# Expert numbers by one wide mask in place of sixteen compare-sums, in a three-block kernel on one core

## The chip, the cores and the metric

The kernel runs on one core of a Trainium2 chip. The core has five engines that run their own instruction streams in order: TensorE (PE in the rows, with PEld for its weight loads), VectorE (DVE), ScalarE (ACT), GpSimd (POOL) and SyncE (SP, which starts most transfers). The metric is the device time of one execution in microseconds, as the median of several runs.

## What is computed

Three blocks of a sequence model run one after the other on 512 tokens of 1024 features, in float32. The change lies in the second block, in the choice of experts. A token has 8 heads; each head scores 128 keys twice, keeps the 16 best of either list, forms all sums of two, keeps the 16 best sums, and turns their places into numbers of experts out of 16384. Each expert is a row of `peer_u` and a row of `peer_v`.

```python
v1, i1 = lax.top_k(s1, PEER_TOPK)          # 16 of 128 keys
v2, i2 = lax.top_k(s2, PEER_TOPK)
cand = (v1[..., :, None] + v2[..., None, :]).reshape(T, PEER_HEADS, PEER_TOPK * PEER_TOPK)
cand_id = (i1[..., :, None] * N_KEYS + i2[..., None, :]).reshape(T, PEER_HEADS, PEER_TOPK * PEER_TOPK)
score, pos = lax.top_k(cand, PEER_TOPK)
ids = jnp.take_along_axis(cand_id, pos, axis=-1)
gates = jax.nn.softmax(score, axis=-1)
...
act = jax.nn.gelu(jnp.einsum('pd,phkd->phk', hb, expert_u[ib]))
return jnp.einsum('phk,phkd->pd', gb.astype(hb.dtype) * act, expert_v[ib])
```

## The kernel before

The 512 tokens are four tiles of 128, taken in two halves of two tiles. The halves run one behind the other: while half 0 is with its experts, half 1 goes through the first two blocks; while half 1 is with its experts, half 0 goes through the third block. So the experts of a half always run beside dense products of the other half.

**Routing.** `peer_route` (L1061) makes the scores of a half, two heads at a time, with products on TensorE. `route_steps` (L1242) holds what follows for two heads of a token tile. `first` (L1252) calls `top16` (L1232) for each key list: a search for eight largest (L1235), their places (L1236), the list without them (L1238, into the tile `mrep`), and the same once more (L1239, L1240). `cands` (L1267) converts the places to float32 (L1273), multiplies those of the first list by 128 (L1276) and forms the 50 sums of two that can be among the 16 best, first of the values, then of the numbers: nine additions for each (L1281, L1284), over two heads at once or over one. `second` searches the 16 best of the 50 sums and their places. `ids` (L1301) finds the numbers: for each of the 16 places k, one instruction (L1303) compares the row 0..49 (`io`) with the place, multiplies by the 50 numbers and leaves the sum over the columns in an accumulator, which a second small instruction reads. L1306 converts the 16 numbers into `idx`. `soft` makes the gates. All of these are on DVE but an exponential on ScalarE. There are 32 heads in all (8 heads, 4 token tiles), so 512 compare-sums, and 18 calls of `cands` (14 for two heads, 4 for one).

**Experts.** `gather_steps` (L1155) makes 256 steps for a token tile. `fetch` (L1164) lets GpSimd start an indirect transfer of 128 rows of 4 KB, with the numbers from one column of `idx`; up to eight are under way ahead of their use. A step with a row of `peer_u` is a product-sum of 1024 columns on DVE (L1171); a step with a row of `peer_v` is a multiply-add of 1024 columns on DVE (L1194) or, for a share of them, two products on TensorE (L1188).

**What sets the order.** The steps of routing and experts are a list (`self.fill`), merged at even rates. Phases of the other half call `tick` with an amount of work, and steps are let in as a credit grows; a step of the routing counts 0.8, one of the experts 1.46, as before and after the change. Within that, a scheduler of the framework orders the instructions of every engine by its own estimate of durations, so the order on an engine moves when instructions become longer or fewer.

Of the kernel before, what the change touches and what calls it, by code (L numbers as in the profile page):

```python
# [19 lines left out]
P = 128  # L20
T = 512
NT = 4          # token tiles
NH = 2          # token tiles of a half: the halves run one behind the other
# [11 lines left out]
# Costs of steps, in the unit of tick and idle: a transfer of 512 KB, a step of the routing, the end of a token tile  # L35
DMA, ROUTE, FINISH = 1.46, 0.8, 6.0
AHEAD = 8           # gathers under way ahead of their use
GB = 15             # their buffers
# the hidden blocks of the feed-forwards that run piece by piece in the gaps of the other half
ASIDE1 = (4, 4, 4, 4, 4, 2)  # L40
ASIDE3 = (4,) * 4
FIRST3 = 16          # hidden blocks of the third feed-forward of half 0 beside the last experts
ADA = 28             # tiles of the modulation beside the first feed-forward, the others beside the second
CONV_PE = (0, 2)     # blocks of the long convolution on TensorE, by half
# by phase: pace of the steps of the experts, share of their sums that TensorE takes
ZONE = dict(x=(1, 0.5), g=(1, 0.35), h=(1.15, 0.41), c=(0.43, 0.4), f=(1.43, 0), m=(1.73, 0.06), d=(1.09, 0.4),
            R=(1.09, 0.39), r=(1.33, 0.3), F3=(1.1, 0), s=(1, 0.65))
# pieces let in by gap of TensorE
GAP = dict(_0=4, l=3, h=0.74, c=0.22, m=5.53, d=0.9, r=0.5, s=1.6, _4=5.2, ln=8, l4=8)
NORM = 4.82          # pace of a normalisation  # L50
WEIGHTS = 3          # of a tile of weights in float32
# rates of the steps: modulation beside the two feed-forwards, experts during the routing
RATE_ADA, RATE_ROUTE = (0.85, 0.6), (0.92, 2.17)
# the course of the phases beside the experts, the transfers of their own, and the share of the experts' steps to fit in
# [3 lines left out]
class Ker:  # L58
    def __init__(self, ctx, tc, I):
# [3 lines left out]
        self.exact = False      # products in float32 itself, not in parts  # L63
# [14 lines left out]
        self.aux = nc.gpsimd        # for what VectorE need not do, unless GpSimd has transfers to start  # L78
# [3 lines left out]
        # states: of the first and of the second block, then both of the third block's retention  # L82
# [13 lines left out]
    def xt(self, es, side=None):  # L96
        """transposed activations, split in two, for one phase"""
        xp = es.enter_context(self.tc.tile_pool(name="xt", bufs=1, side=side))
        self.XH, self.XL = self.pair(xp, "X", KD)

    def pair(self, pool, name, n, **k):
        """an operand of products, n blocks: in two parts, or whole"""
        if self.exact:
            return pool.tile([P, n, TH], F32, name=name + "H", **k), None
        return [pool.tile([P, n, TH], F32R, name=name + c, **k) for c in "HL"]
# [19 lines left out]
    def course(self, i):  # L125
        """the rate that spreads the steps of the experts over a phase"""
        whole, loads, share = COURSE[i]
        self.rate, self.credit = (share * sum(f[0] for f in self.fill) + loads) / whole, 0.0

    def tick(self, d, load=0.0):  # L130
        """a phase goes on by d, with load for a transfer of its own: the steps of the other half's experts
        go in between so that the transfers are even"""
# [12 lines left out]
    def idle(self, d):  # L145
        """TensorE has little to do for d: pieces of the feed-forward set aside go in between"""
        if self.side is not None:
            self.lull += d
            while self.lull > 0.0 and self.side is not None:
                self.lull -= self.next_piece()  # L150
# [25 lines left out]
    def rsqrt(self, out, in_, scale, eps):  # L176
        """out = (in_ * scale + eps) ** -0.5: Newton's iteration from the halved exponent"""
# [43 lines left out]
    def ahead(self):  # L221
        """of the weights of a feed-forward set aside, split the next tile and load on"""
# [9 lines left out]
    def whole(gen):  # L232
        """all pieces of a generator at once; its value"""
# [12 lines left out]
    def g_fm(self, srcs):  # L246
        """feature-major blocks: out[f, i, t] = sum_k w_i[k, f] X[t, k]; srcs [128, 8*128]"""
# [16 lines left out]
    def g_tm(self, srcs, lhs, evac):  # L264
        """token-major: out[t, c] = sum_k lhs[k, t] w[k, c]; srcs: list of [128, 2, 512]; lhs(k) -> (H, L) [128, 512]"""
# [23 lines left out]
    def stats(self, y):  # L289
        """mean and variance over the free axis (1024 or 512)"""  # L290
# [12 lines left out]
    def g_transpose_x(self, src, scale=None, bias=None):  # L303
        """XH, XL <- split of (src^T * scale + bias); src(t, k) -> [128 t, 128 feat]"""
# [18 lines left out]
    def layer_norm(self, gname, bname, alpha):  # L323
        """x <- alpha * LN(x); XT <- split of LN(x)^T"""
# [35 lines left out]
    def g_ffn(self, parts, up, down, scale, fb=0):  # L360
        """x += scale * ffn; up(pool, j): generator of blocks j and j + 1 of the hidden layer, [128, 2, TH];
        down(k, c): weights of blocks k and k + 1"""
# [164 lines left out]
    def _hgrn(self, hp, uT, acc):  # L527
# [5 lines left out]
        # lower bound: softmax over the two rows, first row  # L533
# [128 lines left out]
    def ada_setup(self):  # L662
        """modulation vectors, feature-major: mod[:, 8*i + k] = feature 128*k + p of the i-th of six"""
# [24 lines left out]
    def wide(self, pool, name, key, n=D, at=0):  # L688
        """a row on all partitions; where transfers hold the time, from its columns on TensorE"""
# [6 lines left out]
    def bcast_row(self, out, colsv):  # L696
        """out[*, 128*k + p] = colsv[p, k]"""
# [18 lines left out]
    def g_rms_xt(self, xn, scale, bias):  # L716
        """xn[t] <- x * rstd; XT <- split of (xn^T * scale + bias)"""
# [29 lines left out]
    def softplus(self, pool, z, n):  # L747
        """z <- log(1 + exp(z)), accurate for any z"""
# [17 lines left out]
    def gemm_narrow(self, pool, src, n, meta=None):  # L766
        """token-major X @ w[:, :n] -> psum [128, (t, n)]; src [128, 8*n]; with the meta tokens from 256 on"""
# [22 lines left out]
    def _mixer2(self, mp):  # L790
# [5 lines left out]
        # q, k, v: short convolution and silu, feature-major  # L796
# [32 lines left out]
    def put_mix(self, blk, t, src, nb=4, dst=None):  # L829
        """XH, XL blocks blk.. of token tile t <- split of src^T (src token-major [128, nb*128])"""  # L830
# [41 lines left out]
    def delta_gates(self, dp, ab):  # L872
        nc, I = self.nc, self.I
        # g = -exp(a_log) * softplus(a + dt_bias), beta = sigmoid(b)
# [13 lines left out]
    def _delta(self, dp, qkv, zz, g, bt):  # L888
# [12 lines left out]
        eg = dp.tile([P, 3, NH, 4], F32, name="eg")   # exp of the sums of g: up to here, all, after here  # L901
# [6 lines left out]
        for t in range(NH):  # L908
# [30 lines left out]
            # decay, transposed: DT[j, i] = exp(sum of g over j < tau <= i) for j <= i, else 0  # L939
# [18 lines left out]
            # q exp(gc) feature-major; k exp(total - gc), kb exp(gc) token-major  # L958
# [11 lines left out]
            # X = (I + A)^-1 by doubling over block sizes, with its transpose  # L970
# [28 lines left out]
            # u = X (v beta);  wT = -(X (kb exp(gc)))^T  # L999
# [37 lines left out]
    def head_norm(self, pool, po, gate, blk, t, dst=None):  # L1037
        """XT blocks blk..blk+3 of tile t <- (rms over each head of 128) * gate"""
# [13 lines left out]
    CW = [16 // (i + 1) for i in range(16)]     # of the sorted sums v1[i] + v2[j] only (i + 1)(j + 1) <= 16 can lead  # L1052
# [8 lines left out]
    def peer_route(self, rate):  # L1061
        """experts and gates of this half; leaves in self.fill the steps that gather and apply them"""
# [7 lines left out]
        with ExitStack() as e2:  # L1070
# [7 lines left out]
            # before the first gathers GpSimd has time  # L1078
# [37 lines left out]
            def each(sc, h):  # L1116
                # the first head of the first tile at once, so that its gathers start
# [21 lines left out]
        # the choice for two heads more beside the products of the heads before  # L1139
# [3 lines left out]
        # the last sums of the first tile beside the first products of the second  # L1143
# [6 lines left out]
    def merge(a, b):  # L1150
        """the two lists of steps, in between one another at an even rate"""
# [3 lines left out]
    def gather_steps(self, t, y, h2, idx, gate):  # L1155
# [72 lines left out]
        # those that the first 2, 4, 6 and 8 heads allow  # L1228
# [3 lines left out]
    def top16(self, src, val, idx, n):  # L1232
        """the 16 largest of src [128, n] with their places, in order"""
# [3 lines left out]
        w = self.sm.tile([P, P], F32, tag="mrep", name="mrep", bufs=2)  # L1237
# [4 lines left out]
    def route_steps(self, g, sc, idx, gate, early=False):  # L1242
        """expert numbers and gates of a token tile for heads 2g and 2g + 1, from their scores sc"""
# [3 lines left out]
        NC = self.NC  # L1247

# [7 lines left out]
        def begin():  # L1256
            w = pp.tile([P, 192 + 5 * NC], F32, name="rt", bufs=2)
            o = 0
            st["fx"] = w[:, 0:64].rearrange("p (h i) -> p h i", i=16)
            o = 64  # L1260
            for k, i in (("score", 16), ("pos", 16), ("fp", 16), ("fid", 16), ("cand", NC), ("cid", NC)):
                st[k] = w[:, o:o + 2 * i].rearrange("p (h i) -> p h i", i=i)
                o += 2 * i
            st["jk"] = w[:, o:o + NC]
            st["pos"] = st["pos"].bitcast(U32)

        def cands(h0, h1):  # L1267
            if h0 == 0:
                begin()
            n = h1 - h0  # L1270
            bs, hs = slice(2 * h0, 2 * h1), slice(h0, h1)
            val, fx, cand, cid = st["val"][:, bs, :], st["fx"][:, bs, :], st["cand"][:, hs, :], st["cid"][:, hs, :]
            nc.vector.tensor_copy(fx, st["ix"][:, bs, :])  # L1273
            v1, v2 = val[:, 0::2, :], val[:, 1::2, :]
            f1, f2 = fx[:, 0::2, :], fx[:, 1::2, :]
            nc.vector.tensor_scalar(f1, f1, 128.0, None, op0=ALU.mult)  # L1276
            for dst, a, b in ((cand, v1, v2), (cid, f1, f2)):
                o = 0
                for i in range(8):
                    w = self.CW[i]  # L1280
                    nc.vector.tensor_tensor(out=dst[:, :, o:o + w], in0=b[:, :, 0:w],  # L1281
                                            in1=a[:, :, i:i + 1].to_broadcast([P, n, w]), op=ALU.add)
                    o += w
                nc.vector.tensor_tensor(out=dst[:, :, o:o + 8], in0=a[:, :, 8:16],  # L1284
# [669 lines left out]
```

## Time and profile before

| | |
|---|---|
| median of three runs | 3475.92 us |
| the three runs | 3460.99, 3475.92, 3478.14 us |
| span of the profiled execution | 3464.7 us |
| mean granted TensorE clock | 0.932 of full speed |
| DMA over the span | 957.1 MB, mean 276 GB/s |

The profile gives the span of one execution, from its first to its last instruction, and no other time of that execution. Of the runs, one is shorter than this span and two are longer. [...] The accumulator's read stands as an instruction of its own (DVE_READ_ACCUMULATOR).

### The profile page before, as it was taken

To read this page: it belongs to the slowest core of one execution; us is meant where nothing else is said; L and a number is where in the kernel's file an instruction comes from. 1 tells how busy PE (TensorE), PEld (TensorE's weight loads), DVE (VectorE), ACT (ScalarE), POOL (GpSimd) and SP (SyncE) were. 2 spreads that over 40 slices of the span, in tenths; PEclk is the share of its full clock that TensorE was granted. 3 is DMA by queue.
4 is the path that set the end of the run, shared out by engine and by line. 5 is a ranking of instruction groups with operands and counts; after the bars stand their busy time and mean duration, and the time that the engine had idled before them with its cause. 6 is when DMAs were issued, how large, how long until landed. Compare 5 with 4: busy or idle time off the path is not lost. (4 is left out here: it accounts for less than half of the span.)

```text
span 3464.7 us, 44842 instructions
## 1 busy us (share of the span) xinstructions
PE 3023.7 (87%) x15402; PEld 2350.9 (68%) x15402; DVE 2667.9 (77%) x6456; ACT 1145.3 (33%) x1687; POOL 1439.0 (42%) x1187
## 2 busy tenths in 40 slices
PE   9999999998979789987777867879797975999998
PEld 9987889888866357836354643536474745888897
DVE  7779686665588999878898999897877786566555
ACT  4454544553312242103222121112222213455554
POOL 0020000023245656655677567586767671211200
PEclk9999999999999899998899988899998987999999
DMA  8863477542389979998999899999999995644365
GB/s 312 279 194 118 131 267 233 168 161 86 105 303 357 355 263 384 409 402 325 381 326 375 335 339 391 347 368 357 333 365 359 396 409 193 182 133 139 119 188 162
DMA packets 276757, 957.10 MB, mean 276 GB/s; under 512 B 38304, under 2 KB 42144, under 8 KB 276528
## 3 DMA queue, kind: packets, MB, share of 16 engines
q0 software_dynamic: 147456, 536.94, 41.0%
q1 hardware_dynamic: 129072, 417.29, 35.6%
q8 instruction: 122, 2.00, 0.2%
q14 instruction: 107, 0.88, 0.1%
HBM read 947.81 MB, written 2.10 MB: 274 GB/s over the span
## 5 line engine op out<-in xcount | busy, mean ns | idle before, releaser
L1164 POOL DMA_INDIRECT gu<-in_peer_v,idx x512 | 633.6, 1238 | 317.1 <-issue 111.9
L1164 POOL DMA_INDIRECT gu<-in_peer_u,idx x512 | 609.3, 1190 | 349.6 <-issue 110.9
L1171 DVE SCALAR_TENSOR_TENSOR gu<-gu 128x1024 f32<-128x1024 f32 x512 | 620.7, 1218 | 59.4 <-DMA gu<-in_peer_u,idx 55.7
L203 DVE TENSOR_TENSOR wL<-wr,wH 128x1024 fp32r<-128x1024 f32 x332 | 409.1, 1234 | 249.2 <-ACT wH L202 231.9
L256 PE MATMUL ps<-XH,wr 128*128 128x256 f32 x2368 | 528.7, 383 | 0.2 <-issue 0.2
L256 PEld LDWEIGHTS ps<-XH,wr 128*128 128x128 f32 x2368 | 450.9, 192 | 73.2 <-issue 12.8
L202 ACT CAST wH<-wr 128x1024 fp32r<-128x1024 f32 x332 | 348.3, 1050 | 440.3 <-PE ps L281 217.4
L1194 DVE SCALAR_TENSOR_TENSOR gu<-gu,act 128x1024 f32<-128x1024 f32 x366 | 467.6, 1278 | 28.6 <-DMA gu<-in_peer_v,idx 23.4
L1188 PE MATMUL ps<-gu,dg 128*128 128x512 f32 x568 | 306.5, 664 | 101.8 <-DMA gu<-in_peer_v,idx 67.4
L1188 PEld LDWEIGHTS ps<-gu,dg 128*128 128x128 f32 x568 | 112.7, 212 | 206.9 <-issue 158.2
L278 PE MATMUL ps<-wr,XH 128*128 128x512 f32 x512 | 229.1, 601 | 0.0
L256 PE MATMUL ps<-XH,wH 128*128 128x256 f32 x1408 | 206.5, 289 | 16.3 <-ACT XH L116 10.0
L256 PE MATMUL ps<-XH,wL 128*128 128x256 f32 x1408 | 202.4, 287 | 1.5 <-DVE wL L203 1.2
L256 PE MATMUL ps<-XL,wH 128*128 128x256 f32 x1408 | 203.0, 288 | 0.2
L256 PEld LDWEIGHTS ps<-XH,wH 128*128 128x128 f32 x1408 | 186.6, 196 | 21.9 <-ACT XH L116 13.7
L256 PEld LDWEIGHTS ps<-XH,wL 128*128 128x128 f32 x1408 | 185.6, 196 | 2.9 <-DVE wL L203 2.7
L203 DVE TENSOR_TENSOR fL<-fr,fH 128x1024 fp32r<-128x1024 f32 x98 | 126.1, 1288 | 79.5 <-ACT fH L202 50.1
L256 PEld LDWEIGHTS ps<-XL,wH 128*128 128x128 f32 x1408 | 186.5, 197 | 0.6 <-DVE XL L118 0.6
L278 PEld LDWEIGHTS ps<-wr,XH 128*128 128x128 f32 x512 | 98.0, 193 | 122.7 <-issue 120.3
L202 ACT CAST fH<-fr 128x1024 fp32r<-128x1024 f32 x98 | 102.6, 1047 | 175.4 <-PE ps L256 58.7
L1186 ACT ACTIVATE dg<-ident,act 128x128 f32<-128x128 f32 x142 | 55.1, 400 | 312.3 <-PE ps L1188 246.5
L184 POOL TENSOR_TENSOR r<-rx,mhalf 128x1 f32<-128x1 f32 x18 | 11.9, 669 | 330.7 <-DVE rx L182 330.7
(618 smaller groups left out, 5462.4 us busy)
## 6 DMA issues: line engine op xcount, KB each, us to landing
wr<-in_wi_fm SPq DMA_DIRECT2D x112, 512.0 KB
wr<-in_wi_tm SPq DMA_DIRECT2D x96, 512.0 KB
wr<-in_wf SPq DMA_DIRECT2D x96, 512.0 KB
wr<-in_wo SPq DMA_DIRECT2D x64, 512.0 KB
wa<-in_wada SPq DMA_DIRECT2D x48, 512.0 KB
wr<-in_f2g SPq DMA_DIRECT2D x44, 512.0 KB
wr<-in_f2u SPq DMA_DIRECT2D x44, 512.0 KB
wr<-in_f2d SPq DMA_DIRECT2D x44, 512.0 KB
```

The source lines that it names most:

```text
L184: nc.gpsimd.tensor_tensor(out=out, in0=x, in1=self.mhalf[:p, :].to_broadcast(list(out.shape)), op=ALU.pow)
L202: self.nc.scalar.copy(H, raw)
L203: self.nc.vector.tensor_tensor(out=L, in0=raw, in1=H, op=ALU.subtract)
L256: nc.tensor.matmul(ps[:, i * TH:(i + 1) * TH], a[:, k * P:(k + 1) * P], b[:, k, :], start=n == 0, stop=n == KD * len(terms) - 1)
L278: nc.tensor.matmul(pss[t], lh[:, ts], wh, start=k == 0, stop=k == nk - 1)
L1164: nc.gpsimd.indirect_dma_start(out=g, out_offset=None, in_=I[src], in_offset=bass.IndirectOffsetOnAxis(ap=idx[:, s:s + 1], axis=0))
L1171: nc.vector.scalar_tensor_tensor(g, g, 1.0, h2, op0=ALU.mult, op1=ALU.mult, accum_out=st["act"][:, s:s + 1])
L1186: nc.scalar.activation(dg, self.ident, AF.Copy, scale=c)
L1188: nc.tensor.matmul(st["ps"][i], dg, g[:, i * 512:(i + 1) * 512], start="pe" not in st, stop=s == 127)
L1194: nc.vector.scalar_tensor_tensor(st["acc"], g, c, st["acc"], op0=ALU.mult, op1=ALU.add)
```

## The change

`cands` converts the places in place (in the second half of the tile `rv`), so that values and places lie in one tile, and forms the sums of both by the same instruction: nine additions over twice the columns in place of eighteen. The results lie in one tile `cc`, values first, numbers second. `ids` makes a mask of 16 x 50 for a head by one comparison (the row 0..49 repeated for each place, against each place repeated over 50 columns), multiplies it by the 50 numbers repeated, and sums over the columns: three instructions over 800 columns (L1305, L1306, L1307 of the changed file) in place of sixteen pairs. The mask has one buffer (`eq`); the tile of the searches, `mrep`, has one buffer in place of two, and the scratch tile `rt` becomes smaller. Costs and tables that pace the steps are the same; the other lines of the diff are comments that went.

```diff
-        w = self.sm.tile([P, P], F32, tag="mrep", name="mrep", bufs=2)
+        w = self.sm.tile([P, P], F32, tag="mrep", name="mrep", bufs=1)
...
-            w = pp.tile([P, 192 + 5 * NC], F32, name="rt", bufs=2)
+            w = pp.tile([P, 128 + 4 * NC], F32, name="rt", bufs=2)
...
-            nc.vector.tensor_copy(fx, st["ix"][:, bs, :])
-            v1, v2 = val[:, 0::2, :], val[:, 1::2, :]
-            f1, f2 = fx[:, 0::2, :], fx[:, 1::2, :]
+            nc.vector.tensor_copy(rv[:, 1, bs, :], st["ix"][:, bs, :])
+            f1 = rv[:, 1, bs, :][:, 0::2, :]
             nc.vector.tensor_scalar(f1, f1, 128.0, None, op0=ALU.mult)
-            for dst, a, b in ((cand, v1, v2), (cid, f1, f2)):
-                o = 0
-                for i in range(8):
-                    w = self.CW[i]
-                    nc.vector.tensor_tensor(out=dst[:, :, o:o + w], in0=b[:, :, 0:w],
-                                            in1=a[:, :, i:i + 1].to_broadcast([P, n, w]), op=ALU.add)
-                    o += w
-                nc.vector.tensor_tensor(out=dst[:, :, o:o + 8], in0=a[:, :, 8:16],
-                                        in1=b[:, :, 0:1].to_broadcast([P, n, 8]), op=ALU.add)
+            both, dst = rv[:, :, bs, :], st["cc"][:, :, hs, :]
+            a, b = both[:, :, 0::2, :], both[:, :, 1::2, :]
+            o = 0
+            for i in range(8):
+                w = self.CW[i]
+                nc.vector.tensor_tensor(out=dst[:, :, :, o:o + w], in0=b[:, :, :, 0:w],
+                                        in1=a[:, :, :, i:i + 1].to_broadcast([P, 2, n, w]), op=ALU.add)
+                o += w
+            nc.vector.tensor_tensor(out=dst[:, :, :, o:o + 8], in0=a[:, :, :, 8:16],
+                                    in1=b[:, :, :, 0:1].to_broadcast([P, 2, n, 8]), op=ALU.add)
...
         def ids(h):
-            for k in range(16):
-                nc.vector.scalar_tensor_tensor(st["jk"], io, st["fp"][:, h, k:k + 1], st["cid"][:, h, :],
-                                               op0=ALU.is_equal, op1=ALU.mult, accum_out=st["fid"][:, h, k:k + 1])
+            eq = pp.tile([P, 16, NC], F32, name="eq", bufs=1)
+            wide = lambda a: a.rearrange("p (o j) -> p o j", o=1).to_broadcast([P, 16, NC])
+            fp = st["fp"][:, h, :].rearrange("p (k o) -> p k o", o=1).to_broadcast([P, 16, NC])
+            nc.vector.tensor_tensor(out=eq, in0=wide(io), in1=fp, op=ALU.is_equal)
+            nc.vector.tensor_tensor(out=eq, in0=eq, in1=wide(st["cc"][:, 1, h, :]), op=ALU.mult)
+            nc.vector.tensor_reduce(out=st["fid"][:, h, :], in_=eq, op=ALU.add, axis=AX.X)
```

DVE's order before, at the end of the first head of half 0 (`rt` holds sums, places and numbers, `rv` values and places of the keys, `sc` the scores, `idx` the numbers that the gathers read):

```order
L1289 CAST rt<-rt 128x16
L1303 SCALAR_TENSOR_TENSOR rt<-io,rt 128x50 x14
L1235 MAX rv<-sc 128x8
L1303 SCALAR_TENSOR_TENSOR rt<-io,rt 128x50
L1236 MAX_INDEX rv<-rv,sc 128x8
L1303 SCALAR_TENSOR_TENSOR rt<-io,rt 128x50
L1238 MATCH_REPLACE mrep<-rv,sc 128x128
L1306 CAST idx_9031<-rt 128x16
```

The same place on DVE in the changed kernel:

```order
L1288 CAST rt<-rt 128x16
L1305 TENSOR_TENSOR eq<-io,rt 128x800
L1306 TENSOR_TENSOR eq<-eq,rt 128x800
L1307 TENSOR_REDUCE rt<-eq 128x16
L1309 CAST idx_9031<-rt 128x16
L1235 MAX rv<-sc 128x8 x2
```

Sixteen compare-sums with three instructions of the next searches between them became three wide ones with nothing between.

DVE's order before, around the first expert step (L1171), which stands 62 rows behind the first head's numbers:

```order
L1303 SCALAR_TENSOR_TENSOR rt<-io,rt 128x50
L1240 MAX_INDEX rv<-rv,mrep 128x8
L1303 SCALAR_TENSOR_TENSOR rt<-io,rt 128x50
L1171 SCALAR_TENSOR_TENSOR gu,act<-gu 128x1024
L1303 SCALAR_TENSOR_TENSOR rt<-io,rt 128x50
```

The first expert step in the changed kernel, on DVE:

```order
L1236 MAX_INDEX rv<-rv,sc 128x8
L1240 MAX_INDEX rv<-rv,mrep 128x8
L1272 CAST rv<-rv 128x32
L1274 TENSOR_SCALAR rv<-rv 128x16
L1171 SCALAR_TENSOR_TENSOR gu,act<-gu 128x1024
L1280 TENSOR_TENSOR rt<-rv 128x2x16
L1280 TENSOR_TENSOR rt<-rv 128x2x8
```

The first expert step now stands 16 rows behind the first head's numbers, ahead of the second head's sums of candidates, and not among its compare-sums. The orders of GpSimd and SP are the same but for one transfer of SP late in the program.

## Rows read from the trace of the kernel before

**Rows 1.** the page's first part: busy us (share of the span) and instructions of each engine.

```profile
PE 3023.7 (87%) x15402; PEld 2350.9 (68%) x15402; DVE 2667.9 (77%) x6456; ACT 1145.3 (33%) x1687; POOL 1439.0 (42%) x1187
```

**Rows 2.** the windows view: stretch and its us, busy us (instructions) by engine, TensorE clock, DMA.

```profile
950.00:1150.00 200.00, 165.93 (x661) 120.92 (x660) 174.24 (x789) 43.36 (x72) 104.04 (x89) 0.92 0.89 335
1250.00:1550.00 300.00, 285.47 (x1081) 205.26 (x1080) 258.79 (x812) 61.31 (x110) 187.50 (x151) 0.97 0.99 382
1900.00:2050.00 150.00, 111.01 (x471) 80.79 (x470) 142.31 (x641) 32.06 (x63) 88.83 (x76) 0.87 0.89 332
2050.00:2350.00 300.00, 242.60 (x824) 138.04 (x823) 271.30 (x1022) 48.15 (x86) 211.50 (x170) 0.90 0.99 368
```

**Rows 3.** the windows view of line 1303 alone, by the same columns.

```profile
950.00:1150.00 200.00, 25.94 (x192) 0.92 0.89 335
1250.00:1550.00 300.00, 43.14 (x320) 0.97 0.99 382
1900.00:2050.00 150.00, 13.44 (x102) 0.87 0.89 332
2050.00:2350.00 300.00, 54.99 (x410) 0.90 0.99 368
```

**Rows 4.** groups by line and shape: busy us, mean ns of one | idle before, releaser.

```profile
L1303 DVE SCALAR_TENSOR_TENSOR rt<-io,rt 128x50 f32<-128x50 f32 x512 | 133.5, 261 | 13.0 <-remote 7.9 <-DVE rv L1236 1.1 <-DVE mrep L1238 1.0
...
L1303 DVE DVE_READ_ACCUMULATOR rt<-io,rt 128x1 f32 x512 | 40.3, 79 | 0.0
...
L1043 DVE TENSOR_REDUCE ss<-osq 128x4 f32<-128x512 f32 x16 | 10.9, 680 | 8.4 <-ACT osq L1041 7.3 <-issue 1.1
...
L1661 DVE TENSOR_TENSOR xd<-xs,dt 128x512 f32<-128x512 f32 x8 | 5.5, 685 | 0.7 <-ACT xs L1659 0.5 <-issue 0.2
```

**Rows 5.** DVE's timeline at 2108 us: start us, us, engine, line, operation.

```profile
2108.93 1.27 DVE L1194 SCALAR_TENSOR_TENSOR gu<-gu,act 128x1024 f32<-128x1024 f32 x1
2110.13 0.25 DVE L1303 SCALAR_TENSOR_TENSOR rt<-io,rt 128x50 f32<-128x50 f32 x1
...
2110.32 0.14 DVE L1281 TENSOR_TENSOR rt<-rv 128x4 f32<-128x4 f32 x1
...
2111.81 0.26 DVE L1281 TENSOR_TENSOR rt<-rt 128x32 f32<-128x32 f32 x2
2112.00 0.25 DVE L1303 SCALAR_TENSOR_TENSOR rt<-io,rt 128x50 f32<-128x50 f32 x1
```

**Rows 6.** DVE's timeline at 2229 us.

```profile
2229.47 0.68 DVE L1531 TENSOR_TENSOR kf<-kf,rw__17082 128x512 f32<-128x512 f32 x1
2230.07 0.26 DVE L1303 SCALAR_TENSOR_TENSOR rt<-io,rt 128x50 f32<-128x50 f32 x1
```

**Rows 7.** DVE's timeline over the first head of half 0.

```profile
953.90 0.49 DVE L1235 MAX8 rv<-sc 128x8 f32<-128x128 f32 x2 [11.44 <-ACT sc L1103]
...
957.07 0.67 DVE L1281 TENSOR_TENSOR rt<-rt 128x16 f32<-128x16 f32 x8
...
959.61 0.27 DVE L1303 SCALAR_TENSOR_TENSOR rt<-io,rt 128x50 f32<-128x50 f32 x1
...
959.93 0.27 DVE L1303 SCALAR_TENSOR_TENSOR rt<-io,rt 128x50 f32<-128x50 f32 x1
...
965.00 0.16 DVE L1306 CAST idx<-rt 128x16 uint32<-128x16 f32 x1
```

**Rows 8.** DVE's waits from 1250 to 1550 us: total us, times, longest us.

```profile
DVE gu L1171 <- DMA gu<-in_peer_u,idx: 30.1, 16, 16.5
```

**Rows 9.** GpSimd's timeline at the first gathers.

```profile
965.47 1.24 POOL L1164 DMA_INDIRECT gu<-in_peer_u,idx  x1 [12.87 <-DVE rv L1235]
967.01 0.96 POOL L1164 DMA_INDIRECT gu<-in_peer_u,idx  x1 [0.30 <-issue]
...
994.64 1.99 POOL L1164 DMA_INDIRECT gu<-in_peer_v,idx  x1 [0.30 <-issue]
```

**Rows 10.** DVE's timeline at its first expert step.

```profile
984.40 1.22 DVE L1171 SCALAR_TENSOR_TENSOR gu<-gu 128x1024 f32<-128x1024 f32 x1
```

More of the change, by code (lines that the diff above doesn't have):

```diff
@@ L1256, in begin @@
         def begin():
-            w = pp.tile([P, 192 + 5 * NC], F32, name="rt", bufs=2)
+            w = pp.tile([P, 128 + 4 * NC], F32, name="rt", bufs=2)
             o = 0
[L1259 to L1264, printed above, removed]
+            for k in ("score", "pos", "fp", "fid"):
+                st[k] = w[:, o:o + 32].rearrange("p (h i) -> p h i", i=16)
+                o += 32
+            st["cc"] = w[:, o:].rearrange("p (k h i) -> p k h i", k=2, i=NC)
             st["pos"] = st["pos"].bitcast(U32)
@@ L1271, in cands @@
             bs, hs = slice(2 * h0, 2 * h1), slice(h0, h1)
-            val, fx, cand, cid = st["val"][:, bs, :], st["fx"][:, bs, :], st["cand"][:, hs, :], st["cid"][:, hs, :]
-            nc.vector.tensor_copy(fx, st["ix"][:, bs, :])
-            v1, v2 = val[:, 0::2, :], val[:, 1::2, :]
-            f1, f2 = fx[:, 0::2, :], fx[:, 1::2, :]
+            nc.vector.tensor_copy(rv[:, 1, bs, :], st["ix"][:, bs, :])
+            f1 = rv[:, 1, bs, :][:, 0::2, :]
             nc.vector.tensor_scalar(f1, f1, 128.0, None, op0=ALU.mult)
-            for dst, a, b in ((cand, v1, v2), (cid, f1, f2)):
-                o = 0
-                for i in range(8):
-                    w = self.CW[i]
-                    nc.vector.tensor_tensor(out=dst[:, :, o:o + w], in0=b[:, :, 0:w],
-                                            in1=a[:, :, i:i + 1].to_broadcast([P, n, w]), op=ALU.add)
-                    o += w
-                nc.vector.tensor_tensor(out=dst[:, :, o:o + 8], in0=a[:, :, 8:16],
-                                        in1=b[:, :, 0:1].to_broadcast([P, n, 8]), op=ALU.add)
+            both, dst = rv[:, :, bs, :], st["cc"][:, :, hs, :]
[8 more added lines that the diff above has]
+                                    in1=b[:, :, :, 0:1].to_broadcast([P, 2, n, 8]), op=ALU.add)
         def second(h):
-            self.top16(st["cand"][:, h, :], st["score"][:, h, :], st["pos"][:, h, :], NC)
+            self.top16(st["cc"][:, 0, h, :], st["score"][:, h, :], st["pos"][:, h, :], NC)
             nc.vector.tensor_copy(st["fp"][:, h, :], st["pos"][:, h, :])
```

## The prediction

> **What bounds the kernel now.** I read the page's busy shares first [rows 1]: TensorE is busy 87% of the span, DVE (VectorE) 77%, and a mean says nothing yet about the stretch that the edit touches. All edited instructions belong to the choice of experts, so the second view is a table of the four stretches in which line 1303 runs [rows 3], and beside it all engines in the same stretches [rows 2]. There DVE is busy for 174 of 200, 259 of 300, 142 of 150 and 271 of 300 us, which is more than TensorE in three of the four. From 950 to 1150 some 11.4 of the 26 idle us of DVE lie ahead of the first head's search, as it waits for its scores [rows 7]. So DVE sets the pace nearly everywhere, with one exception: from 1250 to 1550 TensorE is busy for 285 of 300 us, the DMA share is 0.99 at 382 GB/s, and DVE waits 30.1 us for gathered rows [rows 2, 8]. A faster DVE gains little there. From 2050 to 2350 the DMA share is 0.99 too, but at 368 GB/s, so a part of that stretch has room. The third view is DVE's timeline, because it gives what an instruction really occupies: the time from its start to the start of the next one, its pitch, which is shorter than its duration.
>
> **Compare-sums removed.** A head had sixteen of them on 50 columns, 512 in all. Their durations are 261 ns and 79 ns for the accumulator read behind each [rows 4], together 174 us. But they overlap their neighbours. One that starts at 2110.13 lets the next instruction start at 2110.32: a pitch of 0.19 us, accumulator read included, since that runs under the neighbour [rows 5]. Where they stand one behind the other, as in the first head, the pitch is 959.93 - 959.61 = 0.32 us [rows 7]. The order puts nearly all of them between other work, so I take 512 x 0.19 + 16 x 0.13 = 99 us. The windows of line 1303 sum to 137.5 us [rows 3], which counts tails that overlap other instructions; that is the upper bound.
>
> **Wide operations added.** Three per head, 96 in all, each over 16 x 50 = 800 columns. No such row exists before, so I bound it: a product of two SBUF operands over 512 columns has a pitch of 2230.07 - 2229.47 = 0.60 us [rows 6], an expert sum over 1024 columns one of 2110.13 - 2108.93 = 1.20 us [rows 5]. On the straight line between them 800 columns cost 0.60 + 0.60 x 288/512 = 0.94 us; both ends are kept for the range. Broadcast operands don't change it (a product of 512 columns with one takes 685 ns), nor does a reduction (680 ns for 512 columns) [rows 4]. So 96 x 0.94 = 90 us are added, and 58 to 115 us are the ends. The edit of the expert numbers is therefore worth only 99 - 90 = 9 us of DVE time by the values I take, where durations would promise far more.
>
> [...]
>
> **Sums of candidates merged.** 18 calls had 18 small additions each, now 9: 162 fewer, with the same columns in total. Two of 32 columns have a pitch of (2112.00 - 2111.81)/2 = 0.095 us [rows 5]; eight of 5 columns on average (16 to 2) take 0.67 us, and (0.67 - 0.14)/7 = 0.076 us each, where 0.14 is the duration of one [rows 5, 7]. So the part that doesn't depend on columns is about 0.07 us, and 162 x 0.07 = 11 us go (5 to 20 us). That the candidate values now wait for the conversion and the product with 128 costs two small operations of latency in a head, some 0.15 us, with other instructions between.
>
> **One buffer for the search.** The changed order can no longer interleave the two searches of a head. In the worst case each of the 96 searches exposes two waits between dependent operations; the nearest row is the back-to-back pair of compare-sums, whose pitch of 0.32 us is 0.05 above 0.19 plus 0.08. That makes 0 to 10 us; the order still places other work between most of them, so I take 2 us. The eq tile's single buffer costs nothing while all its users are on the in-order DVE; were that cover gone, it would be one wide operation's wait per head.
>
> **First gathers.** GpSimd stands still for 12.87 us before the first gather, until the first head's numbers are there [rows 9]. From 959.61 to 965.00 that is 5.39 us of compare-sums [rows 7]; three wide operations make 2.8 plus some 0.2 us of waits. With the merged sums the gathers start 3 us earlier, of which about 1 us is in the DVE terms already. The second half starts in the same way: 2 x 2 = 4 us.
>
> **Sum.** DVE gives back 9 + 11 - 2 = 18 us. How much of it reaches the end is read from the stretches, weighted by line 1303 [rows 3]: 950 to 1150 (19%) and 1900 to 2050 (10%) pass it fully, 2050 to 2350 (40%) half, 1250 to 1550 (31%) a quarter, as DMA and TensorE are full there. That makes 0.57 x 18 = 10 us, with the 4 us of the starts 14 us. The profiled execution has a span of 3464.7 us, 11.2 below the median of the runs, 3475.92 (they reach from 3461.0 to 3478.1, so nothing visible lies around the span). 14 us below the median is **3462 us**. About 0.5%, 17 us, is what a measurement of this kernel can tell from no change, so this forecast lies within it, though near its edge.
>
> **Rivals.**
> - *Durations count, not pitches.* Then 174 us go and 96 x 1.01 come (685 ns for 512 columns, 1.27 us for 1024 [rows 4, 5]), 77 us less, and the merged sums give 162 x 0.14 = 23 us; 0.57 x 100 + 4 = 61 us, 3415. For it: line 1303 heads no wait, so its durations look like plain work. Against: next starts lie 0.07 us before the ends all over the timeline. Chance 0.12.
> - *All of it passes.* DVE is busy over 90% of two stretches; freed time anywhere moves the whole interleaved course. 18 + 4 = 22 us, and up to 30 with the lower bound of the wide ones: 3452. Chance 0.11.
> - *Nothing passes.* Gathers at a DMA share of 0.99 and TensorE take the gain as new waits of DVE: 3476. Chance 0.12.
> - *Gather issue is held up: slower.* A gather's issue takes 0.96 us on GpSimd beside small operations, 1.99 us beside a run of 1024-column ones on two SBUF operands [rows 9]. 64 of the wide operations are of that kind, and could add 64 x 1.0 us. GpSimd is busy 211.5 of 300 us from 2050 to 2350, and 170 issues with a gap of 0.30 us make it 262: 38 us are free [rows 2, 9]. Some 26 such operations fall there, so they fit unless they meet the bursts; it decides once half of the 64 us reaches gathers that DVE waits for: +32 - 14, 3494 us. Chance 0.08. [...]
> - *The products' columns weigh more.* 800 columns three times stand for 50 columns sixteen times. If the removed sums cost 0.11 us (the 0.19 without the accumulator's 0.079 [rows 4]), 56 us go and 90 come: 34 more, less 9 for the rest, times 0.57: 14 us slower, 3490, and beyond 3493 with any price above. Against: the accumulator read is part of the pitch in the rows. Chance 0.04. [...]
> - *The order moves.* In the new order the first expert step stands 16 rows behind the first numbers, ahead of the second head's sums. It began 984.40 - 965.47 = 18.9 us after the first gather's issue, without a wait [rows 9, 10]; if a gather needs the 16.5 us of the longest wait [rows 8], DVE idles some 13 us at either start: +26 - 14, 3488. Chance 0.09.
>
> **Numbers.** The forecast has 0.44, of which 0.15 beyond the bound of 17 us and 0.29 inside. Faster: 0.15 + 0.12 + 0.11 = 0.38. Same: 0.29 + 0.12 + half of the last two rivals, 0.06 = 0.47. Slower: 0.08 + 0.07 = 0.15. The range, 3432 to 3492, takes in all cases but the first rival and the worst ends of the fourth and fifth.
>
> **What would show it.** Right: 96 wide rows of about 1.0 us whose pitch is 0.94; DVE instructions down by 512 sums, 512 reads and 162 additions, up by 96, to 5366; DVE busy near 2640; the first gather some 3 us nearer to the first search; a DVE wait for gathers from 1250 to 1550 that grows. Wrong: a wide pitch above 1.1 us, gather issues of some 2 us throughout the routing stretches, a DVE wait of over 10 us ahead of the first expert step, or DVE busy lower by 60 us and more.

## The result, and the profile after

The changed kernel takes 3506.97 us (median of four runs, 3495.02 to 3512.67), the kernel before 3469.20 us beside it (3460.99 to 3478.14): a ratio of 1.0106, 95% interval 1.0079 to 1.0132. It is slower by some 37 us, and the time lies above the forecast's range. The profiled execution took 3507.06 us with a span of 3505.3.

The page's first part and the same four windows as in [rows 1, 2], now of the changed kernel:

```profile
PE 3027.3 (86%) x15402; PEld 2352.2 (67%) x15402; DVE 2645.7 (75%) x5366; ACT 1145.8 (33%) x1687; POOL 1444.8 (41%) x1187
```

```profile
950.00:1150.00 200.00, 167.44 (x653) 120.12 (x652) 167.28 (x557) 41.27 (x69) 99.68 (x88) 0.91 0.88 331
1250.00:1550.00 300.00, 263.74 (x1056) 199.21 (x1055) 253.13 (x511) 67.24 (x124) 183.79 (x146) 0.94 0.92 356
1900.00:2050.00 150.00, 125.57 (x482) 84.56 (x480) 137.74 (x450) 32.35 (x63) 95.32 (x81) 0.93 0.96 376
2050.00:2350.00 300.00, 239.14 (x824) 135.81 (x824) 266.86 (x656) 53.85 (x97) 217.50 (x167) 0.88 0.98 361
```

DVE has the 5366 instructions that were forecast and is busy 22.2 us less than in [rows 1]. So the loss is not in the cost of the edited instructions. The second window says where to look first: from 1250 to 1550 us TensorE is busy 263.74 us where it was 285.47 [rows 2], and the DMA share is 0.92 where it was 0.99. The windows hold the same times and not quite the same work, since the changed kernel runs later there.

The wide operations in the groups by line and shape, against the compare-sums of [rows 4]:

```profile
L1305 DVE TENSOR_TENSOR eq<-io,rt 128x800 f32<-128x800 f32 x32 | 31.4, 980 | 0.0
L1306 DVE TENSOR_TENSOR eq<-eq,rt 128x800 f32<-128x800 f32 x32 | 31.3, 978 | 0.0
L1307 DVE TENSOR_REDUCE rt<-eq 128x16 f32<-128x800 f32 x32 | 31.1, 972 | 0.0
```

DVE's timeline over the first head of half 0 and one wide operation between other work, against [rows 7]:

```profile
954.81 0.49 DVE L1235 MAX8 rv<-sc 128x8 f32<-128x128 f32 x2 [11.34 <-ACT sc L1103]
...
960.98 0.99 DVE L1305 TENSOR_TENSOR eq<-io,rt 128x800 f32<-128x800 f32 x1
962.00 0.99 DVE L1306 TENSOR_TENSOR eq<-eq,rt 128x800 f32<-128x800 f32 x1
963.03 0.98 DVE L1307 TENSOR_REDUCE rt<-eq 128x16 f32<-128x800 f32 x1
964.05 0.17 DVE L1309 CAST idx<-rt 128x16 uint32<-128x16 f32 x1
...
969.80 1.27 DVE L1171 SCALAR_TENSOR_TENSOR gu<-gu 128x1024 f32<-128x1024 f32 x1 [1.91 <-DMA gu<-in_peer_u,idx]
...
978.92 0.97 DVE L1306 TENSOR_TENSOR eq<-eq,rt 128x800 f32<-128x800 f32 x1
979.81 0.18 DVE L1297 TENSOR_TENSOR gate<-gate,gsum 128x32 f32<-128x32 f32 x1
```

A wide operation has a pitch of 962.00 - 960.98 = 1.02 us behind its own predecessor, 979.81 - 978.92 = 0.89 us between others. Over all 96 the median is 0.90 us.

**Where the loss begins.** I set the start of each TensorE product of the changed kernel against that of the same product before. Up to 950 us they are within 3 us of each other; behind that the changed kernel is late, by 17 us at 1040 us, 23 at 1160, 34 at 1300, 39 at 1315, and from then to the end nearly always by 35 to 51. Slower products do not make it: the granted TensorE clock is 0.927 over this execution and 0.932 before, but along the dense products from 1324 to 1414 us the lag stays at 39.0 us. Everything is lost between some 985 and 1315 us, in the routing of half 0 and the first block of half 1 behind it. There DVE's timeline of the changed kernel shows this among the last key searches:

```profile
1044.13 1.27 DVE L1194 SCALAR_TENSOR_TENSOR gu<-gu,act 128x1024 f32<-128x1024 f32 x1
...
1045.59 1.20 DVE L1171 SCALAR_TENSOR_TENSOR gu<-gu 128x1024 f32<-128x1024 f32 x1
...
1046.79 0.27 DVE L1238 MATCH_REPLACE8 mrep<-rv,sc 128x128 f32<-128x128 f32 x1
1046.98 1.27 DVE L1194 SCALAR_TENSOR_TENSOR gu<-gu,act 128x1024 f32<-128x1024 f32 x1
1048.17 0.28 DVE L1239 MAX8 rv<-mrep 128x8 f32<-128x128 f32 x1
1048.38 1.20 DVE L1171 SCALAR_TENSOR_TENSOR gu<-gu 128x1024 f32<-128x1024 f32 x1
...
1049.79 1.20 DVE L1171 SCALAR_TENSOR_TENSOR gu<-gu 128x1024 f32<-128x1024 f32 x1
...
1050.99 0.27 DVE L1238 MATCH_REPLACE8 mrep<-rv,sc 128x128 f32<-128x128 f32 x1
```

Between the parts of one search stand expert steps of 1.2 us. Before, the last replace followed the one ahead of it without any:

```profile
1035.76 0.28 DVE L1238 MATCH_REPLACE8 mrep<-rv,sc 128x128 f32<-128x128 f32 x1
...
1036.92 0.28 DVE L1238 MATCH_REPLACE8 mrep<-rv,sc 128x128 f32<-128x128 f32 x1
```

Counted to the last replace of a key search, 31 expert steps stand ahead in the changed kernel, 20 before. SP waits for that replace to start the first loads of half 1, since they go into memory that the routing gives back. SP's waits from 1000 to 1120 us and its timeline, first before, then of the changed kernel:

```profile
SPq L170 <- DVE mrep L1238: 17.4, 1, 17.4
```

```profile
1037.29 0.33 SPq L170 DMA_DIRECT2D gf<-in_ln_g_c  x1
```

```profile
SPq L170 <- DVE mrep L1238: 25.1, 1, 25.1
```

```profile
1051.35 0.33 SPq L170 DMA_DIRECT2D gf<-in_ln_g_c  x1
```

Eleven steps by the pitch of 1.20 us [rows 5] are 13.2 us; the loads start 14.1 us later. In all eighteen traces of this case they start 0.36 to 0.37 us behind the start of that replace. TensorE's first product of half 1's next block (L702) reads the third of them, `grc`, and TensorE stands still for it in the changed kernel:

```profile
1057.17 1.94 PE L702 MATMUL ps<-ident,grc 128*128 128x128 f32 x8 [6.06 <-DMA grc<-in_ln_g_c]
```

Before, this product began at 1039.98 us, 17.2 us sooner. What could put the steps there is the edit I gave the least room: `mrep` with one copy. A search writes it, searches it for the next eight and reads it for their places; with one copy the next search's replace must stand behind that read.

### The profile page after: what moved, and what is told of

Same layout as the page of the kernel before. It is cut to its first block, busy times and chain, and to the rows that moved or that the text cites. A ratio compares the mean times of both kernels' runs of the same rounds, so it can differ in the third digit from the quotient of the medians.

```text
span 3505.3 us, 43787 instructions
## 1 busy us (share of the span) xinstructions
PE 3027.3 (86%) x15402; PEld 2352.2 (67%) x15402; DVE 2645.7 (75%) x5366; ACT 1145.8 (33%) x1687; POOL 1444.8 (41%) x1187
## 5 line engine op out<-in xcount | busy, mean ns | idle before, releaser
L1171 DVE SCALAR_TENSOR_TENSOR gu<-gu 128x1024 f32<-128x1024 f32 x512 | 622.1, 1219 | 81.1 <-DMA gu<-in_peer_u,idx 78.1
L256 PEld LDWEIGHTS ps<-XH,wr 128*128 128x128 f32 x2368 | 450.4, 192 | 81.7 <-issue 21.9
```

The lines of the kernel that those rows point to most:

```text
L256: nc.tensor.matmul(ps[:, i * TH:(i + 1) * TH], a[:, k * P:(k + 1) * P], b[:, k, :], start=n == 0, stop=n == KD * len(terms) - 1)
L1171: nc.vector.scalar_tensor_tensor(g, g, 1.0, h2, op0=ALU.mult, op1=ALU.mult, accum_out=st["act"][:, s:s + 1])
```

## The experiments

Every ratio is against the kernel before on the same chip; the chips differ (3451 to 3474 us for the kernel before), so the ratios are compared and not the times. "Steps" are the expert steps on VectorE ahead of the last key search of half 0, "loads" the start of `gf` counted from the first search, both read from each run's trace. The steps are a matter of the built order. The start of the loads is one reading: of the kernels of e8, e2 and e3 a second execution (e14, e15, e16) has the same steps and loads at 85.2, 83.6 and 83.5 us, so differences of up to some 4 us say little.

| run | copies of mrep | steps | loads, us | ratio | 95% interval |
|---|---|---|---|---|---|
| before | 2 | 20 | 83.4 | 1 | |
| changed | 1 | 31 | 96.5 | 1.0106 | 1.0079 to 1.0132 |
| e1, before with one copy | 1 | 26 | 92.3 | 1.0105 | 1.0091 to 1.0120 |
| e5, one copy in half 0 alone | 1, 2 | 23 | 87.7 | 1.0024 | 1.0012 to 1.0036 |
| e6, one copy in half 1 alone | 2, 1 | 20 | 80.6 | 1.0005 | 0.9994 to 1.0015 |
| e7, e1 with steps held | 1 | 19 | 81.9 | 1.0021 | 1.0011 to 1.0030 |
| e8, changed with steps held | 1 | 19 | 81.0 | 1.0032 | 1.0021 to 1.0043 |
| e9, 12 steps sooner | 2 | 20 | 80.4 | 1.0004 | 0.9995 to 1.0012 |
| e10, 32 steps sooner | 2 | 33 | 98.7 | 1.0084 | 1.0071 to 1.0097 |
| e2, changed with two copies | 2 | 22 | 84.2 | 0.9987 | 0.9975 to 0.9999 |
| e3, numbers alone | 2 | 20 | 81.7 | 0.9972 | 0.9958 to 0.9987 |
| e4, sums alone | 2 | 21 | 85.1 | 0.9983 | 0.9966 to 1.0001 |
| e11, e3 with steps held | 2 | 19 | 80.9 | 1.0003 | 0.9992 to 1.0014 |
| e12, e3 with searches first | 2 | 20 | 77.1 | 0.9995 | 0.9985 to 1.0006 |

**The parts of the change, one at a time.** e1 is before with one word of the diff:

```
-        w = self.sm.tile([P, P], F32, tag="mrep", name="mrep", bufs=2)
+        w = self.sm.tile([P, P], F32, tag="mrep", name="mrep", bufs=1)
```

> The kernel before with one copy of mrep in place of two, nothing else. Buffer theory (the single copy is the loss: a search's replace must wait until the search ahead has read the copy, the searches stand in single file, and 26 + 5 expert steps of half 0 stand ahead of its last key search; in this kernel 23 + 3, against 19 + 1 before): most of the loss is here without any wide operation, 3490 to 3512 us, ratio 1.006 to 1.013, and the loads of half 1 start 8 to 14 us later than the 1037 us of before. Rival, shorter routing (the wide operations and merged sums bring the second head's gathers 11 us earlier, their unbroken run holds up the products): within 0.3% of before, 3460 to 3480.

It measured 1.0105: the whole loss, with every compare-sum and addition of before in place. But TensorE reaches half 1 by another path here: an expert product ahead of L702 waits for gathered rows, until later than the loads, which start at 1045.31 us.

```profile
1050.87 2.05 PE L1188 MATMUL ps<-gu,dg 128*128 128x512 f32 x2 [16.40 <-DMA gu<-in_peer_v,idx]
1052.71 1.92 PE L702 MATMUL ps<-ident,grc 128*128 128x128 f32 x8
```

So the late loads are not the only thing that an order with more expert steps ahead of the searches delays. e2 is the changed kernel with two copies; room comes from letting places, their float form and the numbers share words:

```
-            w = pp.tile([P, 128 + 4 * NC], F32, name="rt", bufs=2)
+            w = pp.tile([P, 64 + 4 * NC], F32, name="rt", bufs=2)
...
+            st["pos"], st["fid"] = st["fp"].bitcast(U32), st["fp"]
```

> The changed kernel with two copies of mrep again; room is made by letting places, their float form and the expert numbers lie in the same words. Buffer theory: 20 + 2 expert steps ahead of the last key search as in before, the loss is gone: 3440 to 3475 us, ratio 0.992 to 1.002. Rival, shorter routing: the second head's gathers are still early and unbroken, so 3495 to 3512, ratio 1.007 to 1.013.

0.9987: the loss is gone. The rival, a routing so short that its gathers come too early, falls with both. e3 keeps two copies and the wide numbers but adds scores and numbers apart, in two loops of nine; e4 keeps the merged sums and puts the sixteen compare-sums back. Of each the core, against the changed kernel:

```
+            for a, b, dst in o2:
...
+                    nc.vector.tensor_tensor(out=dst[:, :, o:o + w], in0=b[:, :, 0:w],
+                                            in1=a[:, :, i:i + 1].to_broadcast([P, n, w]), op=ALU.add)
```

```
+            for k in range(16):
+                nc.vector.scalar_tensor_tensor(st["jk"], io, st["fp"][:, h, k:k + 1], st["cc"][:, 1, h, :],
+                                               op0=ALU.is_equal, op1=ALU.mult, accum_out=st["fid"][:, h, k:k + 1])
```

> The wide expert numbers alone: two copies of mrep, and the sums of scores and of numbers apart as before. Buffer theory: 3445 to 3475 us, ratio 0.993 to 1.002 (by the prediction's terms 9 us of pitch for the numbers, some of it passed on). Rival, shorter routing: 3490 to 3510, since the numbers are where the second head's routing gets short.

> The merged sums alone: two copies of mrep and sixteen compare-sums for the numbers of a head. Buffer theory: 3455 to 3475 us, ratio 0.996 to 1.002 (162 instructions of 0.07 us less on VectorE). Rival, shorter routing: nearly as before, since the sums are the smaller part of the shortening: 3465 to 3485.

Both lie where the buffer theory has them, 0.9972 and 0.9983.

**Which half.** In e5 and e6 the tile's tag and its copies depend on the half (as shown in e5, with `2 - self.hf` in e6):

```
+        w = self.sm.tile([P, P], F32, tag=f"mrep{self.hf}", name="mrep", bufs=1 + self.hf)
```

> The kernel before with one copy of mrep for the searches of half 0 and two for those of half 1. If the loss is made where half 0 is routed (products of TensorE lag 13 us by 1040 and 34 to 39 by 1300 in the run with one copy, and no more later): 3495 to 3512 us, ratio 1.006 to 1.012. If it needs the searches of half 1 too: within 0.3% of before.

> The kernel before with one copy of mrep for half 1 alone. By the place of the lag: within 0.3% of before, 3465 to 3485 us. If the searches of half 1 carry it: 3490 to 3512.

Half 1 is free of it, as expected. Half 0 alone gave 1.0024, far less than I expected: a miss. The table goes with it: in e5 the scheduler let only 23 steps ahead of the last search where e1 has 26, though the edit to half 0 is the same. What it is in the program that makes these two orders differ I did not find. Nor do three steps measure up to the difference: e1 loses some 36 us, e5 some 8. Where no steps are held, their number goes with the sign of the loss and not with its size, since e1 with 26 loses as much as the changed kernel with 31, and more than e10 below with 33.

**The copy or the order.** e7 and e8 keep one copy, and tie the first 60 expert steps recorded behind the last key search to it by an edge that orders issue on VectorE without a wait:

```
+        self.tc.add_manual_dep(ins.ins, self.behind.ins.name,
+                               mybir.DependencyInfo(mybir.DependencyClass.NoSync, mybir.DependencyReason.DATA),
+                               reason="behind the searches")
```

> The kernel before with one copy of mrep, and the first 60 expert steps of half 0 that are recorded behind its last key search are queued behind it on VectorE, so that 18 + 1 expert steps stand ahead of it and not 23 + 3 (19 + 1 before). Order theory (the single copy costs by the steps that slip in ahead of the searches, so that the routing's memory comes free late): 3465 to 3483 us. Rival, waits on the chip (searches in single file take longer whatever stands between): 3495 to 3512. Third, only the 13 us of the first stage come back and the 20 between 1220 and 1300 us stay: 3487 to 3496.

> The changed kernel, one copy of mrep, with the same 60 steps queued behind the last key search: 18 + 1 steps ahead of it and not 26 + 5. Order theory: 3460 to 3480 us. Waits on the chip: 3495 to 3512. First stage alone: 3487 to 3496; the same if the second head's early gathers matter, which stay as they are in the changed kernel.

1.0021 and 1.0032: most of the loss comes back with one copy still in place, more than a first stage of 13 us alone would give. A rest of 0.2 to 0.3% stays. e9 and e10 do the reverse, two copies and the order of the loss, by raising the priority of the first expert steps (32 in e10, as shown; 12 in e9):

```
+            with self.sooner():
                 nc.vector.scalar_tensor_tensor(g, g, 1.0, h2, ...
...
+        return self.tc.high_priority(600) if self.sooners <= 32 else ExitStack()
```

> The kernel before, two copies of mrep, and the first 12 expert steps of half 0 given priority over the searches: 11 of them stand ahead of its 8th key search (none before, 10 in the changed kernel), while 19 + 1 stand ahead of the last as before. If these early steps, which the changed kernel with the steps held still has, are what is left of its loss there (0.3%): ratio 1.002 to 1.006. If not: 0.998 to 1.002.

> The same with the first 32 expert steps: 27 + 6 stand ahead of the last key search of half 0 (26 + 5 in the changed kernel, 19 + 1 before), with two copies of mrep and every instruction of before. Order theory (the place of the expert steps is enough for the loss, whatever the cause of the place): ratio 1.006 to 1.013, and the loads of half 1 start 8 to 14 us later. Waits on the chip (the single copy itself costs): 0.997 to 1.003.

e10 has every instruction of before and two copies, and is slower by 0.84%. SP's timeline in e9 and then in e10, on the same chip:

```profile
1031.96 0.33 SPq L170 DMA_DIRECT2D gf<-in_ln_g_c  x1
```

```profile
1048.80 0.33 SPq L170 DMA_DIRECT2D gf<-in_ln_g_c  x1
```

The loads start 16.8 us later; the searches began 1.5 us earlier. e9, with 11 steps ahead of the eighth search but none more ahead of the last, measures 1.0004. So it is the place of the last key search that costs, not expert steps early in the routing as such. Whether the late loads alone do it, or also the expert numbers that a later routing delays, is not separated: no run moved the loads by themselves.

**Ending the searches sooner.** e11 holds the steps in e3, e12 gives the key searches of half 0 a little priority there:

```
+                with self.tc.high_priority(60) if self.hf == 0 else ExitStack():
                     self.top16(sc[:, b, :], st["val"][:, b, :], st["ix"][:, b, :], P)
```

> The wide numbers alone with two copies, and the steps recorded behind the last key search of half 0 queued behind it: 18 + 1 stand ahead of it in place of 19 + 1. Order theory: a step or so is 1 to 2 us of the loads' start, 0.995 to 0.998, not to be told from the numbers alone (0.9972). Any other: the same.

> The wide numbers alone with two copies, the key searches of half 0 given a little priority: 13 + 0 steps ahead of its 12th search in place of 16 + 0, 17 + 0 ahead of its 20th in place of 18 + 1, 19 + 1 ahead of the last as before. If the end of the searches alone counts: 0.995 to 0.999, as the numbers alone. If every step ahead of a search costs: 0.992 to 0.996. If the expert steps are needed early, since their buffers let the gathers go on: 0.999 to 1.004.

1.0003 (0.9992 to 1.0014) and 0.9995 (0.9985 to 1.0006). In e12 the loads start 77.1 us behind the first search, 3.3 us sooner than in e9 on the same chip, and nothing is gained. As far as one trace with so small a difference can say, the path is lengthened by a late end of the searches and not shortened by an early one.

**On one chip.** The last four runs put the changed kernel, e8, e2 and e3 side by side.

> The changed kernel as it is, beside the three that follow on one chip, since the runs so far came from chips whose times for the kernel before were 3451 to 3474 us. Order theory: ratio 1.008 to 1.012 again.

> The changed kernel with the steps held. If the order of the expert steps is the whole loss, as the kernel with two copies, 0.997 to 1.000; if the single copy costs something of its own, 1.002 to 1.004 again, with two copies below it by 0.3% or more on the same chip.

> The changed kernel with two copies. If the wide numbers and merged sums are worth what the prediction summed before its order terms (some 12 us): 0.996 to 0.999. If their gain is hidden by other work: 0.9995 to 1.002.

> The wide numbers alone with two copies. If their gain passes: 0.996 to 0.999 as on the slower chip. If it is hidden, as the two kernels made from it suggested (1.0003 and 0.9995 on a faster chip): 0.9995 to 1.001.

1.0115 (1.0087 to 1.0143), 1.0032 (1.0013 to 1.0051), 1.0000 (0.9982 to 1.0019) and 0.9981 (0.9962 to 1.0000). The rest of 0.3% with one copy and the steps held repeats, with the two-copy kernel below it by the same amount. Its place is not settled: one copy in half 1 alone cost nothing (e6). Nor is it shown to be the copy's. e11 is the hold without the single copy: it gave 1.0003 where the same kernel without the hold gave 0.9972 (e3) and 0.9981 (e16). That is 0.2 to 0.3% too, so holding the steps may cost this much by itself; but e3 did not run on the chip of e11, and the chip may be the reason.

**How 14 us become 37.** TensorE's waits from 1100 to 1360 us, before and in the changed kernel:

```profile
PE ps L604 <- ACT kT L598: 12.0, 1, 12.0
PE ps L835 <- DVE osq L1047: 8.5, 1, 8.5
...
PE ps L310 <- DVE xres L345: 6.2, 1, 6.2
PE ps L631 <- DVE E L627: 4.4, 4, 2.3
```

```profile
PE ps L631 <- DVE E L627: 28.6, 8, 22.8
PE ps L835 <- DVE osq L1047: 12.2, 2, 11.6
PE ps L310 <- DVE xres L345: 11.9, 2, 11.3
...
PE ps L494 <- issue: 4.3, 5, 2.1
```

The lag grows where half 1 needs DVE: 5 us up to the first product on `E` (a wait of 22.8 us), 3 on `osq`, 5 on `xres`. The largest piece behind the first 17 is the convolution (L494), whose 124 products run from 1241.8 to 1271.1 us before and from 1266.9 to 1306.5 in the changed kernel, 10 us longer. Its line, in the changed kernel and in e10:

```profile
L494 PE MATMUL ps<-uT,cdg x124: 377/379/795, 1266.9 to 1306.1; 128*128 128x256 f32 x124
```

```profile
L494 PE MATMUL ps<-uT,cdg x124: 377/378/634, 1259.0 to 1289.9; 128*128 128x256 f32 x124
```

e10 comes as late to it, 28 us behind e9 where the changed kernel is 25 behind the kernel before, but takes 31 us, and ends at 1.0084; e1 takes 41 us, near the 40 of the changed kernel, whose second execution (e13) takes 42. In the other fifteen traces of this case it takes 28.6 to 31.5 us. In the changed kernel ScalarE, which makes the diagonals for these products, shows two loads of function tables and then gaps without a visible releaser:

```profile
1282.43 1.28 ACT L1174 ACT_TABLE_LOAD   x1
...
1285.19 1.28 ACT L1293 ACT_TABLE_LOAD   x1
...
1292.82 0.40 ACT L493 ACTIVATE cdg<-ident,cw 128x128 f32<-128x128 f32 x1 [2.43 <-remote]
```

Gates and activations of the experts, let in at another time, fall into the convolution there. That is not enough to explain it: in e10 the same two loads (its L1182 and L1303) fall into the convolution, and no such gap follows. What lengthens it stays open. ScalarE's timeline in e10:

```profile
1277.09 1.28 ACT L1182 ACT_TABLE_LOAD   x1
...
1279.49 1.28 ACT L1303 ACT_TABLE_LOAD   x1
...
1282.10 7.31 ACT L493 ACTIVATE cdg<-ident,cw 128x128 f32<-128x128 f32 x17 [0.21 <-PE ps L494]
```

A lag at 1315 us also need not last. In the profiled executions e5 is 21 us behind e6 on the same chip there and 6 at the end, e10 behind e9 31 and 19 (29 by the medians of the runs); the changed kernel keeps its 39. Why it keeps them was not found. These pieces are read from the traces; none was taken out by an experiment.

## Why the prediction was wrong

**The step that failed is "One buffer for the search".** I priced the single copy as waits between dependent operations, 0 to 10 us, and took 2 because "the order still places other work between most of them". That other work is the cost. The instructions between are expert steps of 1.2 us, eleven more of them ahead of the last search, and what stands behind the last search is the memory for half 1's loads, which start 14.1 us later. By e1 the copy costs 1.05%, some 36 us; by e7, e8 and e10 most of that is the order and not the copy. How 14 us grow to 36 is read from the traces and in part open. I asked how long a search would take, and not who waits for the last one.

**Compare-sums and wide operations: right.** 5366 instructions as forecast, DVE busy 2645.7 us against "near 2640", a pitch of 0.89 to 1.02 us against 0.94. With the order as before the numbers alone gave 0.9972 and 0.9981, while e11 and e12, made from them, gave 1.0003 and 0.9995 on a faster chip: 0 to 10 us, as the 9 us of DVE time that I took allow, and far from the 61 us of the rival that counts durations. That rival falls, and so does the one by the columns of the products.

**Sums merged: no more than their size.** The merged sums alone measure 0.9983 (0.9966 to 1.0001), some 6 us where I had 11 us of DVE time, and not clear of nothing. The two edits together with two copies gave 0.9987 and 1.0000, so what each gives does not seem to add up; with two steps more ahead of the last search than before, that kernel's order differs too.

**First gathers: nearly right.** The first gather's numbers come 964.05 - 954.81 = 9.2 us behind the first search, against 11.1 before [rows 7]: 2 us nearer where I said 3.

**Pass-through: the sign was not in the sum.** I let 57% of DVE's gain pass and no delay. In e12 an earlier end of the searches gained nothing; e10 shows that a later one costs more than itself: 16.8 us at the loads became 29 (0.84%).

**The gather rival fell.** I gave the hold-up of GpSimd 0.08. By the median its issues are as long as before: line 1164 before and then after, minimum, median and maximum in ns:

```profile
L1164 POOL DMA_INDIRECT gu<-in_peer_u,idx x512: 932/1014/3615, 965.5 to 2832.9; - x171
```

```profile
L1164 POOL DMA_INDIRECT gu<-in_peer_u,idx x512: 932/1002/7441, 964.5 to 2875.0; - x171
```

The medians, 1014 ns and then 1002, show no hold-up of the issues. GpSimd as a whole is busy 1444.8 us against 1439.0 [rows 1]. This rival stood at 3494 us, outside the range that I said took in all but its worst ends.

**"The order moves" had the right sign and the wrong mechanism.** It let DVE idle 13 us for gathers ahead of the first expert step. DVE waited 1.91 us there (969.80), and e9 shows that eleven steps ahead of the eighth search cost nothing. The order moved at the other end of the routing, and by the buffer. The chance of 0.09 went to a story about the first head, where the last one decides.

## What to carry to other kernels

Where a scheduler orders the instructions, giving up a copy of a scratch tile is not priced by the waits on it: ask what the scheduler will put into them, and what is waiting for the last instruction of that chain. Count in the built order how many long steps stand ahead of the instruction that frees a pool, before and after; here eleven steps of 1.2 us told the sign, though not the size. And when a change comes with a saving elsewhere to make room, try that saving alone first: one word of this diff carried all of its loss.

## What the runs showed of the hardware

From 1283 to 1308 us of the changed kernel, ScalarE and TensorE both show short gaps without a visible releaser ("remote", "issue"): ScalarE loses 4.9 us in 6 gaps (3.4 us in 2 and 1.5 in 4), TensorE's weight loads 6.9 us in 6. GpSimd starts 15 gathers one behind the other there, with only 0.3 us between. In the same products before, GpSimd waited 12.5 us for a buffer and TensorE had one gap of 0.4 us. An unbroken run of gathers is not enough to make the gaps: in e10's convolution 17 gathers start with the same 0.3 us between, and its products wait for nothing but ScalarE's diagonals, 2.5 us in all. What causes the gaps was not tried.
